# One table load, six pieces of gamma and a first store in two halves, in an RMSNorm that repeats its rows

## The chip, the cores and the metric

One core of one Trainium2 chip. The metric is the time of one execution on the device in microseconds (us), as the median of several; before the change it was 239.42 us (3 runs, 239.32 to 239.43). The span in a profile is about 1.8 us shorter than the time of the same run (237.9 and 239.72 us for the kernel before).

## The reference

(shortened)

```python
def reference(x, gamma):                       # x: 8 x 512 x 2048, gamma: 2048, both f32
    x_rep = np.repeat(x, 2, axis=1)            # every row twice
    rms = np.sqrt((x_rep ** 2).mean(axis=-1, keepdims=True) + 1e-6)
    return (x_rep / rms * gamma[None, None, :]).astype(np.float32)
```

33.6 MB are read and 67.1 MB written.

## The kernel before

Eight tiles of 128 partitions x 4 rows. A tile buffer has room for the eight output rows of a partition; the four input rows are loaded into its second half, normalised, and copied. SyncE issues every load of x and every store, ScalarE issues the loads of gamma and takes squares and roots, GpSimd copies gamma to all 128 partitions, VectorE scales, and each of the two copies half of the repeats. Three tile buffers are used in turn.

```python
    rows = ctx.enter_context(tc.tile_pool(name="rows", bufs=3))
    # ... cut
    def square(i, k):                            # ScalarE: sum of squares, then its root
        # ... cut
        nc.scalar.activation(out=sq[:], in_=ys[i][:, K * (R - 1) + k, :], func=Act.Square, accum_out=ss[:])
        nc.scalar.activation(out=rms[:], in_=ss[:], func=Act.Sqrt, scale=inv_d, bias=eps_t[:])
    # ... cut
    def compute(i):
        for k in range(K):
            scale(i, k, square(i, k))            # VectorE: reciprocal, then y * rstd * gamma_b
        repeat(i, 0, K // 2, nc.scalar.copy)
        repeat(i, K // 2, K, nc.vector.tensor_copy)

    load(0, nc.sync, parts=2)
    gamma_b = singles.tile([P, D], f32, name="gamma_b")
    cuts = [0, *range(D // 4, D + 1, D // 8)]    # seven pieces: 2 KB and six of 1 KB
    for c0, c1 in zip(cuts, cuts[1:]):
        nc.scalar.dma_start(out=gamma_b[0:1, c0:c1], in_=gamma[c0:c1].partition_broadcast(1))
    nc.gpsimd.partition_broadcast(out_ap=gamma_b[:], in_ap=gamma_b[0:1, :])
    # ... cut
    load(1, nc.sync)
    load(2, nc.sync)
    loads_after = {2: (3, 4, 5), 4: (6, 7)}
    for i in range(ntiles):
        compute(i)
        store(i, 0, K)
        for j in loads_after.get(i, ()):
            load(j, nc.sync)
```

Of the kernel before, what the change touches and what calls it, by code (L numbers as in the profile page):

```python
# [1 line left out]

# [4 lines left out]


@with_exitstack
def kernel(  # L10
    ctx: ExitStack,
    tc: tile.TileContext,
    x: bass.AP,
    gamma: bass.AP,
    out: bass.AP,
):
    nc = tc.nc
    P = nc.NUM_PARTITIONS
    f32 = mybir.dt.float32
    Act = mybir.ActivationFunctionType  # L20
    Alu = mybir.AluOpType

    B, S, D = x.shape
    Bo, So, Do = out.shape
    R = So // S
    assert R == 2 and D == Do and B == Bo and So == S * R
    eps = 1e-6
    inv_d = 1.0 / float(D)


    K = 4
    N = B * S
    assert N % (P * K) == 0
    ntiles = N // (P * K)
    x_t = x.rearrange("b s d -> (b s) d").rearrange("(n p k) d -> n p k d", p=P, k=K)
    out_t = out.rearrange("b s d -> (b s) d").rearrange("(n p j) d -> n p (j d)", p=P, j=K * R)

    singles = ctx.enter_context(tc.tile_pool(name="singles", bufs=1))
    rows = ctx.enter_context(tc.tile_pool(name="rows", bufs=3))
    junk = ctx.enter_context(tc.tile_pool(name="junk", bufs=1, space=bass.MemoryType.PSUM))  # L40
    small = ctx.enter_context(tc.tile_pool(name="small", bufs=8))

    ys = []

    def load(i, eng, parts=1):


        y = rows.tile([P, K * R, D], f32, name="y")
        step = K // parts
        for k in range(0, K, step):  # L50
            at = K * (R - 1) + k
            eng.dma_start(out=y[:, at : at + step, :], in_=x_t[i, :, k : k + step, :])
        ys.append(y)

    def store(i, k0, k1):
        nc.sync.dma_start(  # L56
            out=out_t[i, :, R * k0 * D : R * k1 * D],
            in_=ys[i][:, R * k0 : R * k1, :].rearrange("p j d -> p (j d)"),
        )

    def square(i, k):
        sq = junk.tile([P, D], f32, name="sq")
        ss = small.tile([P, 1], f32, name="ss")
        nc.scalar.activation(  # L64
            out=sq[:], in_=ys[i][:, K * (R - 1) + k, :], func=Act.Square, accum_out=ss[:]
        )
        rms = small.tile([P, 1], f32, name="rms")
        nc.scalar.activation(out=rms[:], in_=ss[:], func=Act.Sqrt, scale=inv_d, bias=eps_t[:])  # L68
        return rms

    def scale(i, k, rms):
        rstd = small.tile([P, 1], f32, name="rstd")
        nc.vector.reciprocal(out=rstd[:], in_=rms[:])  # L73
        nc.vector.scalar_tensor_tensor(  # L74
            out=ys[i][:, R * k, :], in0=ys[i][:, K * (R - 1) + k, :], scalar=rstd[:], in1=gamma_b[:],
            op0=Alu.mult, op1=Alu.mult,
        )

    def repeat(i, k0, k1, copy):
        y_r = ys[i].rearrange("p (k r) d -> p k r d", r=R)  # L80
        copy(out=y_r[:, k0:k1, 1, :], in_=y_r[:, k0:k1, 0, :])  # L81

    def compute(i):
        for k in range(K):
            scale(i, k, square(i, k))
        repeat(i, 0, K // 2, nc.scalar.copy)
        repeat(i, K // 2, K, nc.vector.tensor_copy)


    ctx.enter_context(tc.manual_schedule())  # L90
    load(0, nc.sync, parts=2)
    gamma_b = singles.tile([P, D], f32, name="gamma_b")
    cuts = [0, *range(D // 4, D + 1, D // 8)]
    for c0, c1 in zip(cuts, cuts[1:]):
        nc.scalar.dma_start(out=gamma_b[0:1, c0:c1], in_=gamma[c0:c1].partition_broadcast(1))  # L95
    nc.gpsimd.partition_broadcast(out_ap=gamma_b[:], in_ap=gamma_b[0:1, :])  # L96
    eps_t = singles.tile([P, 1], f32, name="eps_t")
    nc.vector.memset(eps_t, eps)  # L98
    load(1, nc.sync)
    load(2, nc.sync)  # L100



    assert ntiles == 8
    loads_after = {2: (3, 4, 5), 4: (6, 7)}
    for i in range(ntiles):
        compute(i)
        store(i, 0, K)
        for j in loads_after.get(i, ()):
            load(j, nc.sync)  # L110


# [1 line left out]
_INS = ['x', 'gamma']  # L114
_OUTS = [((8, 1024, 2048), 'float32')]


# [23 lines left out]
```

## Time and profile before

| | value |
|---|---|
| time | 239.42 us |
| profiled span | 237.9 us |
| VectorE, ScalarE busy | 96.5 us, 101.0 us |
| queue of x and of the stores, share of 16 DMA engines | 98.5% |
| first scaling starts, first store is issued | 14.92 us, 27.05 us |

The lines of the profile that carry the argument are in the prediction below. One view is not shown there: whom SyncE's DMA queue itself waited for (line that waited, what it waited for, us in total, times, longest).

```profile
SPq L52 <- DMA out_dram<-y: 69.6, 5, 19.1
SPq L52 <- DMA y<-in_x_dram: 5.7, 1, 5.7
SPq L52 <- DMA gamma_b<-in_gamma_dram: 0.9, 1, 0.9
```

L52 issues the loads of x. The first row is reuse of tile buffers. The other two cannot be: the first three tiles have fresh buffers, and a load of x needs no gamma. They are waits for a semaphore that a transfer shares with an earlier one. The list of instructions of the built kernel shows eight such semaphores, given to the DMAs in turn; a transfer that is given one again is issued only when the earlier transfer with it has landed.

### The profile page before, as it was taken

Reading aid. Unit: us, or ns where it says so; the run is one execution under the profiler, and the core shown is the slowest. Engines: PE = TensorE matmul, PEld = TensorE weight load, DVE = VectorE, ACT = ScalarE, POOL = GpSimd, SP = SyncE. Lnnn points to the kernel's source line nnn. Section 1 sums busy time; section 2 is a strip of 40 time slices with the busy share of each in tenths; the row PEclk is TensorE's granted clock in tenths of the full one; section 3 lists DMA queues with packets and bytes.
Section 4 is the critical chain, followed back from the end, with each engine's and each line's share of the span. In section 5 each row is a group of like instructions: output and inputs, shape, how many; then the busy total and the mean of one; then the engine's idle time right before and its main releaser. Section 6 shows DMA issues by size and latency. Waiting matters only on the chain.

```text
span 237.9 us, 287 instructions
## 1 busy us (share of the span) xinstructions
DVE 96.5 (41%) x73; ACT 101.0 (42%) x106; POOL 2.5 (1%) x5
## 2 busy tenths in 40 slices
DVE  0049999960000000059999960000199990000000
ACT  2697999900000000099999920000599960000000
POOL 0030000000000000000000000000000000000000
DMA  7999998989899998999998999989998989999994
GB/s 265 436 446 441 441 441 353 530 353 496 386 452 430 397 485 353 441 441 441 441 518 364 464 419 430 452 369 430 435 518 364 518 364 485 397 452 430 408 474 176
DMA packets 2464, 100.69 MB, mean 423 GB/s; under 512 B 279, under 2 KB 285, under 8 KB 286
## 3 DMA queue, kind: packets, MB, share of 16 engines
q1 hardware_dynamic: 2448, 100.66, 98.5%
q14 instruction: 2, 0.02, 0.0%
q10 hardware_dynamic: 14, 0.01, 0.0%
HBM read 33.56 MB, written 67.11 MB: 423 GB/s over the span
## 4 chain that ended last, share of the span: by engine, by line
DMA 58%; ACT 12%; DVE 9%; issue 1%; POOLq 1%; ACTq 1%; SPq 0%
DMA y<-in_x_dram 33%; DMA out_dram<-y 21%; ACT sq L64 8%; DVE y L74 7%; DMA gamma_b<-in_gamma_dram 4%; ACT y L81 3%; DVE y L81 2%; ACT rms L68 1%; POOLq L136 1%; ACTq L95 1%; DVE rstd L73 0%; POOLq L96 0%; SPq L56 0%
## 5 line engine op out<-in xcount | busy, mean ns | idle before, releaser
L64 ACT ACTIVATE sq<-y 128x2048 f32<-128x2048 f32 x32 | 59.7, 1865 | 87.8 <-DMA y<-in_x_dram 87.8
L74 DVE SCALAR_TENSOR_TENSOR y<-y,rstd,gamma_b 128x2048 f32<-128x2048 f32 x32 | 75.3, 2352 | 4.1 <-POOL gamma_b L96 3.0
L73 DVE RECIPROCAL rstd<-rms 128x1 f32<-128x1 f32 x32 | 5.0, 158 | 94.6 <-ACT rms L68 94.3
L81 ACT COPY y<-y 128x4096 f32<-128x4096 f32 x8 | 28.7, 3590 | 1.4 <-DVE y L74 1.4
L81 DVE COPY y<-y 128x4096 f32<-128x4096 f32 x8 | 18.3, 2294 | 0.3
L68 ACT ACTIVATE rms<-ss,eps_t 128x1 f32<-128x1 f32 x32 | 9.4, 295 | 1.0
L64 ACT ACTIVATION_READ_ACCUMULATOR sq<-y 128x1 f32 x32 | 6.0, 187 | 0.0
L64 ACT ACT_TABLE_LOAD x1 | 1.3, 1283 | 3.0 <-issue 3.0
L96 POOL PARTITION_BROADCAST gamma_b<-gamma_b x1 | 2.3, 2294 | 12.2 <-DMA y<-in_x_dram 12.2
L68 ACT ACT_TABLE_LOAD x1 | 1.3, 1283 | 0.0
L98 DVE MEMSET eps_t<- 128x1 f32 x1 | 0.1, 59 | 0.8 <-PEq L125 0.8
L125 POOL MEMSET const-uint8-127<- 128x1 uint8 x1 | 0.1, 102 | 0.0
L125 POOL MEMSET const-bfloat16-1.0<- 128x1 bf16 x1 | 0.1, 101 | 0.0
L125 POOL MEMSET const-float32-0.0<- 128x1 f32 x1 | 0.1, 98 | 0.2 <-issue 0.2
L125 POOL MEMSET const-float32-1.0<- 128x1 f32 x1 | 0.1, 98 | 0.0
## 6 DMA issues: line engine op xcount, KB each, us to landing
y<-in_x_dram SPq DMA_DIRECT2D x7, 4096.0 KB, 14.6
y<-in_x_dram SPq DMA_DIRECT2D x2, 2048.0 KB, 7.4
out_dram<-y SPq DMA_DIRECT2D x8, 24.4
gamma_b<-in_gamma_dram ACTq DMA_DIRECT2D x6, 1.0 KB
gamma_b<-in_gamma_dram ACTq DMA_DIRECT2D x1, 2.0 KB
```

Source lines behind the costliest of these rows:

```text
L64: nc.scalar.activation(out=sq[:], in_=ys[i][:, K * (R - 1) + k, :], func=Act.Square, accum_out=ss[:])
L68: nc.scalar.activation(out=rms[:], in_=ss[:], func=Act.Sqrt, scale=inv_d, bias=eps_t[:])
L73: nc.vector.reciprocal(out=rstd[:], in_=rms[:])
L74: nc.vector.scalar_tensor_tensor(out=ys[i][:, R * k, :], in0=ys[i][:, K * (R - 1) + k, :], scalar=rstd[:], in1=gamma_b[:], op0=Alu.mult, o ...
L81: copy(out=y_r[:, k0:k1, 1, :], in_=y_r[:, k0:k1, 0, :])
L95: nc.scalar.dma_start(out=gamma_b[0:1, c0:c1], in_=gamma[c0:c1].partition_broadcast(1))
L96: nc.gpsimd.partition_broadcast(out_ap=gamma_b[:], in_ap=gamma_b[0:1, :])
L98: nc.vector.memset(eps_t, eps)
L125: nc = _bacc.Bacc("TRN2", target_bir_lowering=False, num_devices=1)
L136: with _tile.TileContext(nc) as tc:
```

## The change

The intent: the square and the root use one function table, loaded at the start; gamma comes in one piece less; the first store need not wait until the whole tile is done.

```diff
     load(0, nc.sync, parts=2)
+
+    nc.scalar.preload_act_table(Act.Sqrt)
     gamma_b = singles.tile([P, D], f32, name="gamma_b")
-    cuts = [0, *range(D // 4, D + 1, D // 8)]
+    cuts = [0, D // 4, *range(D // 2, D + 1, D // 8)]
@@
         compute(i)
-        store(i, 0, K)
+
+        for k0, k1 in ((0, K // 2), (K // 2, K)) if i == 0 else ((0, K),):
+            store(i, k0, k1)
```

## The prediction

> **What bounds the kernel now.** I read the page first: engine shares, the slices, the DMA queues.
>
> ```profile
> DVE 96.5 (41%) x73; ACT 101.0 (42%) x106; POOL 2.5 (1%) x5
> ...
> DMA  7999998989899998999998999989998989999994
> ...
> q1 hardware_dynamic: 2448, 100.66, 98.5%
> q14 instruction: 2, 0.02, 0.0%
> q10 hardware_dynamic: 14, 0.01, 0.0%
> HBM read 33.56 MB, written 67.11 MB: 423 GB/s over the span
> ```
>
> The two compute engines are busy for about 41% of the span. The q1 row, the queue of SyncE with all loads of x and all stores, fills 98.5% of the time of the 16 DMA engines. So 0.985 x 237.9 = 234.4 us of the span is transfer, and only 3.5 us is anything else. Next I asked for busy time in stretches chosen to lie on the phases:
>
> ```profile
> 0.00:1.50 1.50, 0.06 (x1) 0.00 (x0) 0.19 (x4) 1.00 0.00 0
> 1.50:3.00 1.50, 0.00 (x0) 0.02 (x1) 0.00 (x0) 1.00 0.93 220
> 3.00:12.00 9.00, 0.17 (x1) 5.12 (x6) 0.00 (x0) 1.00 1.00 428
> ...
> 31.00:89.00 58.00, 20.04 (x15) 16.98 (x17) 0.00 (x0) 1.00 1.00 434
> 3.00:235.00 232.00, 96.48 (x72) 101.00 (x106) 2.29 (x1) 1.00 1.00 433
> ```
>
> The last two columns are the DMA share and GB/s. From 3 to 235 us the share is 1.00 at 433 GB/s: there is no hole in which a store or a load could have started earlier. In the packet records of the trace the first packet of x begins at 1.74 us and the last packet of a store ends at 236.77 us, 235.03 us apart, against 234.37 us of packet time per engine. All holes inside the stream together are 0.66 us per engine. The first instruction on the queue is issued at 0.72 us, so the rest is 1.0 us from issue to first packet and 1.2 us after the last packet.
>
> The chain of waits, read third, seems to say something else for the start:
>
> ```profile
> 2.69 9.71 DMA gamma_b<-in_gamma_dram
> ...
> 12.55 2.35 POOLq L136
> ...
> 14.92 2.35 DVE y L74
> ...
> 24.69 2.30 DVE y L81
> ...
> 27.05 25.77 DMA out_dram<-y
> 52.82 0.02 issue
> 52.84 48.32 DMA y<-in_x_dram
> ```
>
> It runs through gamma, its broadcast and VectorE to the first store. But the store's 25.77 us are not all transfer: it has 8.39 MB (67.11 MB over 8 stores), which at 434 GB/s is 19.3 us. The other 6.4 us it stands in the queue behind the loads of tiles 1 and 2, about 1 us of it being the issue. The last load of those lands at 33.3 us by its semaphore. So the first store has some 5 us of slack, and the piece of the chain ahead of it is not on the path that sets the end. The chain shows who released whom, not that the engines of the DMA were idle.
>
> **What the Trainium skill says.** "DMA: Bandwidth & Descriptors", Specifications, gives a fabric ceiling of 435 GB/s; the 434 GB/s of 31 to 89 us agrees. It also gives about 358 GB/s for the HBM share of a core; the page's 423 GB/s of reads and writes together is above that, and the measurement decides. The same page, "Issuing engines are not separate DMA queues", says that DMAs issued by ScalarE and SyncE run on the same 16 engines; and "Queues, rings and completion order" says that an engine takes turns between its queue rows packet by packet. The records of q10 agree: 14 packets for seven pieces of gamma, each a data packet and a semaphore packet, and from the second piece on (5.65 us) the two are 0.65 us apart, about one packet of x of 16 KB (0.61 us). "ScalarE: Activation LUTs", "What ACT_TABLE_LOAD costs", gives about 1.28 us for a load and 1.38 us for the drain[...]; the trace has the 1.28 us, but between the end of the first square's read-out (9.94 + 0.19) and the first square root (11.43) there is room for the load alone:
>
> ```profile
> 9.94 0.19 ACT L64 ACTIVATION_READ_ACCUMULATOR sq<-y 128x1 f32 x1
> 10.14 1.28 ACT L68 ACT_TABLE_LOAD   x1
> 11.43 0.29 ACT L68 ACTIVATE rms<-ss,eps_t 128x1 f32<-128x1 f32 x1
> 11.64 1.86 ACT L64 ACTIVATE sq<-y 128x2048 f32<-128x2048 f32 x1
> ```
>
> **The change part by part.** I compared the instruction order of the two built kernels.
>
> Table load. Two loads become one: the square and the square root now share the set loaded first. The load at 10.14 us goes, 1.28 us off ScalarE, so the first square root starts at about 10.15. On the path: nothing. VectorE's first scaling waits for gamma until 14.92, while its reciprocal was done at 11.93.
>
> Gamma. ScalarE loads its table at about 0.72 to 2.0 and issues six pieces after it: in the trace seven took 2.23 us including one of 0.51, so six take 1.7 to 2.0 us and end near 3.9. Before, the first piece (2 KB) got in ahead of x, at 1.62 us, and the other six ran from 5.65 to 12.01, that is 6.36 us. Now all six stand behind x. If their turns start at 5.65 as before, they end at 12.0; if the 1.3 us of later issue carries over in full, at 13.3, and somewhat later when packets of 32 KB (1.21 us) follow those of 16 KB. I take 12 to 14. The broadcast (2.3 us) then ends at 14.9 to 16.5, and tile 0 is done on VectorE 0 to 1.6 us later than before: its last store issue moves from 27.05 to 27.0 to 28.7. All inside the 5 us of slack.
>
> Semaphores. The order list shows eight semaphores given to DMAs in turn. Before, the second half of the first load had to wait for the first piece of gamma (the trace: 0.9 us, issue at 2.03); now gamma comes later in the turn, so both halves go out one after the other near 0.72 and 1.1. The first half has 2.1 MB, 4.8 us of work, so its engines weren't waiting for the second half. Load of tile 1 still waits for the first half to land (8.11). Seven pieces and one store became six and two, so from the second store on every transfer has the same semaphore as before. The sixth piece costs nothing elsewhere.
>
> First store. It goes in two: the first as soon as ScalarE has copied rows 0 and 1 of each partition (19.77 + 3.60 = 23.37, up to 1.6 later), the second when VectorE is done. Both still queue behind load 2. Bytes are the same; 128 packets of 64 KB become 256 of 32 KB. From the packet records: 2.418 us for 64 KB and 1.213 for 32 KB, so two halves cost 8 ns more than one whole. Eight such per engine are 0.06 us, with one more semaphore packet of 9 ns: 0.07 us. The load into that buffer needs the second half to have landed, whose last byte comes in the same place in the stream (52.82 us).
>
> Sum on the end: 0.0 from the table, 0.0 from gamma, +0.07 from packets, and 0 to -0.3 if the start becomes cleaner with ScalarE issuing nothing in the first microsecond. That is 239.42 + 0.07 - 0.1 = about 239.4 us.
>
> **Rivals.**
> 1. The chain is right and the start is on the path: the table load, 1.28 us, and the first half store 3.6 us earlier come off the end. That makes 235.8 to 238.1. For it: the chain of waits. Against it: the DMA share of 1.00 from 3 us on, and the 6.4 us that the first store already stands in the queue. Even if all holes went, only 0.66 us could come.
> 2. Gamma's later issue delays tile 0 beyond the slack. It would have to come more than 5 us later, after 17 us, since everything behind it follows rigidly. For it: gamma takes turns with x on one engine, and turns get twice as long (1.21 us) with tile 1's packets. Six pieces of two turns at 1.21 us would be 14.5 us and end at about 20, 8 us late: an undivided first store would go out at 35, and the stream, whose loads run out near 32.5, would stand still for some 3.5 us. Divided, its first half goes out at 31.4 and its first packet at 32.4, just in time, with 9.7 us of work in it, and the hole is 0 to 1 us: 239.4 to 240.4. Against so late a gamma: 16 packets of 16 KB are in the ring of that engine for the first load, and they last till about 12 us, so few turns are the long ones.
> 3. Shorter store packets cost more than I count: if 32 KB writes behaved as the 16 KB reads (0.611 us each, 1% worse), 0.2 us on 19.3. That would be 239.6.
> 4. The start is cleaner: 0.3 to 0.6 us of the 0.66 us of holes go, 238.9 to 239.1.
>
> **Range and chances.** The runs of before lie within 0.11 us of each other. Rivals 3 and 4 span 238.9 to 239.6; with some difference between chips I take 238.8 to 240.0 for 8 in 10, at 239.4. A change of 2% is 4.8 us: faster by it would need more than all holes of the stream together (chance 0.01), slower by it needs a dry queue of 5 us, far beyond rival 2 (0.02). Within 2%: 0.97.
>
> **What would show it.** In the profile after: one table load of 1.28 us, at the start; the first square root at 10.1 to 10.2; the broadcast starting between 12.3 and 14; the first store's first half issued at 23.4 to 25, the second at 27 to 28.7; the load of tile 3 still issued at about 52.8; q1 at 2,592 packets (2448 + 128 + 16) and again about 98.5%; the share 1.00 in the stretch from 3 to 235. I am wrong if the stretch from 28 to 40 us shows less than full share (rival 2), if the load of tile 3 goes out more than 1 us earlier or later, or if 434 GB/s of the steady stretch changes.

## The result, and the profile after

The changed kernel takes 239.57 us (median of 6 runs, 239.42 to 239.79), the kernel before 239.43 (6 runs, 239.32 to 239.63). The ratio is 1.0006, with a 95% interval of 0.9993 to 1.0019: the same. A ratio, here and below, is the mean time of one kernel's fast runs over that of the other's of the same rounds, so it is not quite the ratio of the medians.

First the page of the kernel after, shares and DMA queues:

```profile
DVE 96.5 (41%) x73; ACT 99.9 (42%) x105; POOL 2.5 (1%) x5
...
q1 hardware_dynamic: 2592, 100.66, 98.6%
q14 instruction: 2, 0.02, 0.0%
q10 hardware_dynamic: 12, 0.01, 0.0%
```

ScalarE lost the 1.1 us of the table load net, the main queue has 144 packets more, gamma's queue two fewer, and the main queue is as full as it was. The stretches (length, busy time of VectorE, ScalarE, GpSimd, TensorE clock, DMA share, GB/s) answer to those of before:

```profile
3.00:12.00 9.00, 0.16 (x1) 3.98 (x4) 0.87 (x1) 1.00 1.00 428
31.00:89.00 58.00, 18.61 (x13) 16.28 (x17) 0.00 (x0) 1.00 1.00 434
3.00:235.00 232.00, 96.46 (x72) 98.66 (x104) 2.29 (x1) 1.00 1.01 432
```

Same share, same rate. What did change is the first tile, in the timeline after (start, duration, engine, line, operation):

```profile
0.72 1.28 ACT L93 ACT_TABLE_LOAD   x1 [0.72 <-PEq L129]
...
0.75 1.93 ACTq L97 DMA_DIRECT2D gamma_b<-in_gamma_dram  x6
...
11.13 2.29 POOL L98 PARTITION_BROADCAST gamma_b<-gamma_b  x1 [10.71 <-DMA gamma_b<-in_gamma_dram]
...
13.46 2.35 DVE L74 SCALAR_TENSOR_TENSOR y<-y,rstd,gamma_b 128x2048 f32<-128x2048 f32 x1 [2.95 <-POOL gamma_b L98]
...
21.93 3.95 SPq L56 DMA_DIRECT2D out_dram<-y  x2
```

The broadcast starts at 11.13 instead of 12.60, the first scaling at 13.46 instead of 14.92, and the store goes out at 21.93 and 25.54 instead of 27.05. So the first tile is 1.5 us ahead, and its first half store 5.1 us. In the chain of waits after, the first store's piece has grown by what the pieces ahead of it lost, and the load of tile 3 follows at 52.96 (before: 52.84):

```profile
25.54 27.36 DMA out_dram<-y
52.96 48.24 DMA y<-in_x_dram
```

The second half holds 4.19 MB, 9.7 us at 434 GB/s, and takes 27.36 us to land. The 1.5 us are given back in the queue, one for one. In the packet records the first packet of x starts at 1.74 us and the last one of a store ends at 236.68 us; before, 1.74 and 236.77. None of the three signs of being wrong that the prediction names came: from 28 to 40 us the share is 0.99, tile 3 goes out 0.12 us later, and the steady rate is 434 GB/s.

### The profile page after: what moved, and what is told of

Its sections match the earlier page's. It is cut to its first block, busy times and chain, and to the rows that moved or that the text cites. A ratio compares the mean times of both kernels' runs of the same rounds, so it can differ in the third digit from the quotient of the medians.

```text
span 237.8 us, 285 instructions
## 1 busy us (share of the span) xinstructions
DVE 96.5 (41%) x73; ACT 99.9 (42%) x105; POOL 2.5 (1%) x5
## 4 chain that ended last, share of the span: by engine, by line
DMA 58%; ACT 12%; DVE 9%; issue 2%; POOLq 1%; ACTq 0%; SPq 0%
DMA y<-in_x_dram 32%; DMA out_dram<-y 22%; ACT sq L64 8%; DVE y L74 7%; DMA gamma_b<-in_gamma_dram 4%; ACT y L81 3%; DVE y L81 2%; ACT rms L68 1%; POOLq L140 1%; ACTq L97 0%; DVE rstd L73 0%; ACT L93 0%; POOLq L98 0%; SPq L52 0%
## 5 line engine op out<-in xcount | busy, mean ns | idle before, releaser
L81 ACT COPY y<-y 128x4096 f32<-128x4096 f32 x8 | 28.7, 3591 | 0.9 <-DVE y L74 0.9
```

The costliest lines, as they stand in the source:

```text
L81: copy(out=y_r[:, k0:k1, 1, :], in_=y_r[:, k0:k1, 0, :])
```

## The experiments

All were run beside the kernel before on the same chip, twelve in four groups. Times are medians; the interval is that of the ratio to the kernel before. Theory A ("stream"): the DMA engines are never empty, so nothing in the first tile counts until it makes them empty. Rival B ("start on the path"): what the chain of waits shows ahead of the first store is paid in full.

**The early table load undone.**

```diff
-    nc.scalar.preload_act_table(Act.Sqrt)
```

> The changed kernel without the early table load, so ScalarE loads two tables again (2 x 1.28 us). Stream theory (the DMA engines are never empty, so work of the first tile costs nothing): first square root back at about 11.3 us instead of 10.02, first scaling still at about 13.5 because gamma gates it, time 239.5 within 0.2 of the changed kernel. Rival, start on the path: 1.3 us more than the changed kernel, 240.8. If gamma's landing was helped by the issue order and not by the number of pieces, the broadcast would move from 11.13 towards 12.6; by the number of pieces it stays at about 11.1.

239.38 us against 239.33, ratio 0.9998 (0.9985 to 1.001). The broadcast and the first root:

```profile
11.27 2.29 POOL L97 PARTITION_BROADCAST gamma_b<-gamma_b  x1 [10.84 <-DMA gamma_b<-in_gamma_dram]
11.38 0.29 ACT L68 ACTIVATE rms<-ss,eps_t 128x1 f32<-128x1 f32 x1
```

The root is late again, and gamma is not; the first scaling starts at 13.59. So the table load is worth nothing to the end, and it is not what brought gamma forward; that leaves the number of pieces. (The build gave out the semaphores differently here too: the load of tile 1 is issued at 2.01 us and not at 7.98. The end did not follow that either.)

**Gamma in seven pieces again.**

```diff
-    cuts = [0, D // 4, *range(D // 2, D + 1, D // 8)]
+    cuts = [0, *range(D // 4, D + 1, D // 8)]
```

> The changed kernel with the seven pieces of gamma of before. If each piece costs two turns of 0.61 to 0.65 us on one DMA engine, the last packet of gamma ends at about 11.8 to 12.0 instead of 10.57, the broadcast starts at about 12.4 and the whole of the first tile moves 1.3 us later: store halves at about 23.2 and 26.9. If instead the early table load brought gamma forward, the broadcast stays at about 11.1. Time by the stream theory 239.5 as before; by the rival (start on the path) 1.3 us more, 240.8.

242.10 us against 239.33, ratio 1.0113 (1.0099 to 1.0127). Neither theory expected this size, and gamma moved the other way: its broadcast started at 8.97 us. Something else had happened. SyncE's waits in this run (same columns as above), and its issues in the timeline near 8 us:

```profile
SPq L52 <- DMA y<-in_x_dram: 6.9, 1, 6.9
```

```profile
0.73 0.38 SPq L52 DMA_DIRECT2D y<-in_x_dram  x1
```

```profile
8.08 0.33 SPq L52 DMA_DIRECT2D y<-in_x_dram  x1
```

Between the first half of the first load, at 0.73, and the second half, at 8.08, SyncE issues nothing. In the built kernel the two halves have the same one of the eight semaphores: the first half takes one, gamma's seven pieces take the other seven, and the second half is given the first again, so it must wait until the first half has landed. By then the stream is empty. Stretches of this run, then of the changed kernel:

```profile
7.75:9.15 1.40, 0.00 (x0) 1.07 (x1) 0.17 (x1) 1.00 0.38 82
```

```profile
7.75:9.15 1.40, 0.00 (x0) 1.16 (x1) 0.00 (x0) 1.00 1.07 457
```

(A packet is counted where it starts, so the share of a short stretch is coarse and can pass 1.) In the packet records no packet of x is in flight from 7.72 to 9.05 us; idle time per engine between 7 and 12 us is about 1.8 us, against none in the changed kernel. The first packets after the pause take 0.7 to 1.4 us instead of 0.61; packet time per engine is 0.6 us more in all. Together 2.4 us, and the span is 2.4 us longer (240.2 against 237.8). This also explains gamma: while x had nothing in the ring (the queue of packets that stand ready for a DMA engine), four pieces went through from 7.54 to 7.74 us, 0.05 us each, where one beside x takes 1.26.

**Seven pieces, but the table load after them.** If the explanation is right, moving one instruction must mend it. Against the previous run:

```diff
-    nc.scalar.preload_act_table(Act.Sqrt)
     # ... cut
     for c0, c1 in zip(cuts, cuts[1:]):
         nc.scalar.dma_start(...)
+    nc.scalar.preload_act_table(Act.Sqrt)
```

> Seven pieces and two half stores as in the run with seven pieces that took 242.1, but the early table load stands after the issues of gamma instead of ahead of them. In the build the second half of the first load then waits for the semaphore of the first piece of gamma (landed at about 2 us), as in the kernel before, and no longer for that of the first half of the same load (landed at 8.1). Shared semaphore theory: no hole near 8 us, the second half issued at about 2.0, gamma's last packet at about 12.0, first scaling near 14.8, time 239.5 (239.2 to 239.9). If seven pieces with two half stores were themselves the cost: 242.1 again.

239.75 us against 239.57, ratio 1.0013 (0.9997 to 1.0029). With the table load behind them, the build gives gamma's first piece its semaphore ahead of the first half, and the second half shares with that piece, which lands early. SyncE's waits and the stretch of before:

```profile
SPq L52 <- DMA gamma_b<-in_gamma_dram: 0.9, 1, 0.9
```

```profile
7.75:9.15 1.40, 0.00 (x0) 1.08 (x1) 0.00 (x0) 1.00 0.93 399
```

Same pieces, same half stores, no hole. It also gives the measure of a piece: from the start of its second piece to the end of its last packet gamma takes 6.37 us with seven pieces (5.54 to 11.91; the same in the kernel before) and 5.14 with six (5.42 to 10.57 in the changed kernel). One piece less is 1.2 us.

**Gamma in one piece.**

```diff
-    cuts = [0, D // 4, *range(D // 2, D + 1, D // 8)]
+    cuts = [0, D]
```

> The changed kernel with gamma in one piece of 8 KB. The first piece has always gone ahead of the first packet of x (1.66 against 1.74 us), so all of gamma should land by about 2.5 to 3 us, the broadcast runs at about 3, the first scaling is gated by the first square root only and starts at about 10.5, the store halves are issued at about 19 and 22.6. Time by the stream theory still 239.4 within 0.2. By the rival (start on the path) 3 us less, 236.5. If one packet of 8 KB cannot go ahead of x, gamma lands at about 6 to 7 us.

239.75 us against 239.33, ratio 1.0016 (1.0003 to 1.0028). Broadcast and first scaling:

```profile
2.86 2.29 POOL L98 PARTITION_BROADCAST gamma_b<-gamma_b  x1 [2.43 <-DMA gamma_b<-in_gamma_dram]
10.76 2.35 DVE L74 SCALAR_TENSOR_TENSOR y<-y,rstd,gamma_b 128x2048 f32<-128x2048 f32 x1
```

The single packet of 8 KB went ahead of x at 1.66 us, as expected, and the first scaling came 4.2 us earlier than in the kernel before. The halves were issued at 21.09 and 22.84; I had expected 19 for the first, and overlooked that ScalarE copies only after its four squares, the third of which waits for the second half load (13.0 us). The end did not gain, and rival B is out.

**No gamma at all** (wrong result: ones in place of gamma).

```diff
-    cuts = [0, D // 4, *range(D // 2, D + 1, D // 8)]
-    for c0, c1 in zip(cuts, cuts[1:]):
-        nc.scalar.dma_start(...)
-    nc.gpsimd.partition_broadcast(...)
+    nc.vector.memset(gamma_b, 1.0)
```

> Wrong result on purpose: gamma is set to ones on VectorE, no transfer and no broadcast. First scaling at about 10.5. Stream theory: 239.4 within 0.3 (8 KB of bytes less count nothing). Rival, start on the path: at least 3 us less, 236.5.

239.77 us against 239.33, ratio 1.0016 (1.0002 to 1.0029), with the first scaling at 10.50. The same verdict. That these two runs lie 0.4 us above the kernel before is more than I expected, and both intervals lie just above 1. The kept traces do not show why: their last store packets end at 236.79 and 236.60 us, against 236.77 in the kernel before. The cause stays open.

**Only the split undone.**

```diff
-        for k0, k1 in ((0, K // 2), (K // 2, K)) if i == 0 else ((0, K),):
-            store(i, k0, k1)
+        store(i, 0, K)
```

> The changed kernel with only the split of the first store undone. The store is issued at about 25.5, and the loads run dry at 31.5 to 32 when no store stands behind them (as the run with the delay of 9.4 us and a whole store showed), so its first packet at 26.5 to 27 is in time by 5 us. Expected 239.4 (239.1 to 239.8), the same as with halves, with 128 x-ring packets fewer. If the halves were worth anything without a delay: above 240.

239.89 us against 239.57, ratio 1.0008 (0.9996 to 1.002); the median is 0.1 us above the range expected. The halves are worth nothing measurable when the first tile is in time.

**How much slack the first store has.** Four runs delay the first tile with idle scalings on VectorE, with the store whole or in halves:

```diff
+            if i == 0 and k == 0:
+                for _ in range(4):               # or 7
+                    nc.vector.scalar_tensor_tensor(out=pad[:], in0=gamma_b[:], scalar=rms[:], in1=gamma_b[:], ...)
```

(The runs with a whole store have the split undone as well, as in the run above.)

Four scalings, store whole:

> The changed kernel with the first store whole, and four idle scalings (about 2.35 us each, 9.4 in all) on VectorE ahead of the first tile's. The store would be issued at about 34.9 instead of 25.5; its first packet starts about 1.0 us later, at 35.9, while load 2 lands at 33.3. Slack theory: the stream has a hole of about 2.6 us, time 242.1 (241.3 to 242.7). If the start is on the path in full: 9.4 more, 248.9. If the slack is larger than I read: 239.5.

Four scalings, store in halves:

> The same delay of 9.4 us with the first store in halves. First half issued at about 31.3, its first packet at 32.3, before load 2 has landed (33.3), and it holds 9.7 us of work, until the second half is issued at 34.9. Slack theory: no hole, 239.5 (up to 239.9): the halves are worth about 2.6 us here. If halves are worth nothing: the same as the whole store with this delay.

Seven scalings, store whole:

> First store whole, delay of seven idle scalings, 16.5 us. Issued at about 42, first packet 43, load 2 landed at 33.3: a hole of 9.7 us, time 249.2 (248 to 250), that is 7.1 more than with the delay of 9.4: past the slack each us of delay costs one us.

Seven scalings, store in halves:

> First store in halves, delay of 16.5 us. First half issued at about 38.4, first packet 39.4, hole of 6.1 us, the second half comes in time behind it: 245.6 (244.6 to 246.5). So the halves are worth 3.6 us once the delay is past both slacks, which is the time between ScalarE's copy and VectorE's last work on the tile.

| delay | store | issued at | stream empty | time, us | ratio to before (95%) |
|---|---|---|---|---|---|
| 9.6 us | whole | 35.21 | 31.87 to 36.06 | 245.05 | 1.0229 (1.0214 to 1.0245) |
| 9.6 us | halves | 31.68, 35.29 | 31.85 to 32.53 | 241.37 | 1.007 (1.0054 to 1.0087) |
| 16.7 us | whole | 42.68 | 32.02 to 43.54 | 252.24 | 1.0531 (1.0515 to 1.0546) |
| 16.7 us | halves | 39.12, 42.73 | 32.10 to 39.97 | 248.62 | 1.038 (1.0365 to 1.0396) |

"Stream empty" is the time in which the packet records show no packet of x or of a store. The stretches of the two runs with the shorter delay, the whole store first:

```profile
32.00:36.00 4.00, 3.93 (x4) 3.94 (x7) 0.00 (x0) 1.00 0.00 0
```

```profile
32.00:36.00 4.00, 3.93 (x4) 3.94 (x6) 0.00 (x0) 1.00 0.92 393
```

The shape came out as expected: past the slack each us of delay costs one us (7.2 us for 7.2), and the halves are worth 3.7 and 3.6 us, the time between the two issues. The sizes were off by 3.0 us and 1.9 us at the shorter delay and by 3.0 us in both runs at the longer one; all four times lie above the ranges expected. Two things were missing. The loads run dry at 31.9 us, not at 33.3: in the kernel before, the last packets of the load (to 33.01 us) share the engines with packets of a store already in the ring (from 32.41 us). Its records have 0.87 us of stretched packets in the ten us from 30 on, against 0.05 in the run with the empty ring. And both delayed runs have about 0.9 us of packet time more than the kernel before, in packets that took up to 3.5 us for 64 KB. They lie near 92 and 122 us with the whole store, near 88 and 119 with the halves, each time at the end of a row of stores or loads, where the other kind follows; the records of before show almost none at these turns. For the whole store: 4.4 us of idle per engine between 25 and 50 us and 0.9 us of longer packets are 5.3 us, and the span is 5.3 us longer. Why those later packets stretch stays open.

**Store packets of 16 KB everywhere.**

```diff
-        for k0, k1 in ((0, K // 2), (K // 2, K)) if i == 0 else ((0, K),):
-            store(i, k0, k1)
+        for h in range(R):                       # R is 2; each transfer: runs of 16 KB, every second one
+            nc.sync.dma_start(
+                out=out_t[i].rearrange("p (a h c d) -> h p a (c d)", a=2, h=2, c=2)[h],
+                in_=ys[i].rearrange("p (a h c) d -> h p a (c d)", a=2, h=2, c=2)[h])
```

> The changed kernel with every store in two transfers, each with runs of 16 KB (four packets where there was one of 64 KB). From the reads' packet times (0.611 us for 16 KB, 2.418 for 64 KB) one run of 64 KB costs 0.026 us more in four pieces; 64 such per engine (56 for the whole stores, and 8 less the 0.008 each for the first) make 1.6 us, with semaphore packets 1.7: 241.2 (240.8 to 241.6). If smaller store packets cost nothing: 239.5. If writes pay more per packet than reads: above 241.6.

240.91 us against 239.47, ratio 1.0056 (1.0042 to 1.007). Of the 4,096 store packets of 16 KB, 4,090 took 0.611 us, as the reads do, so four cost 2.444 against 2.418 us for one of 64 KB: the 0.026 us that I had worked with. The 1.4 us at the end are a little less than the 1.6 to 1.7 worked out from it, near the lower end of the range. The queue of x and of the stores in this run, as its page has it:

```profile
q1 hardware_dynamic: 5648, 100.66, 98.8%
```

With over twice the packets of the kernel before, the cost is 1.4 us. So the 144 packets that the change adds can't be seen.

**Half of the first store left out** (wrong result).

```diff
-        for k0, k1 in ((0, K // 2), (K // 2, K)) if i == 0 else ((0, K),):
+        for k0, k1 in ((K // 2, K),) if i == 0 else ((0, K),):
```

> Wrong result on purpose: the first half of the first store is left out, 4.19 MB of 100.66. If the end is set by the bytes through the 16 engines at 434 GB/s, 9.66 us less than the changed kernel: 229.9 (229.6 to 230.3), if the stream stays without holes: the second half is issued at 25.5, before load 2 has landed. If the end were set by compute or by the chain from the first tile: 239.5.

230.14 us against 239.47, ratio 0.961 (0.959 to 0.963).

```profile
q1 hardware_dynamic: 2448, 96.47, 98.5%
...
HBM read 33.56 MB, written 62.91 MB: 423 GB/s over the span
```

4.19 MB less is 9.3 us less than the kernel before on the same chip (9.4 against the changed kernel), where 9.7 were worked out from 434 GB/s; the four runs spread over 1.1 us, and the profiled span is 9.8 us shorter than that of the changed kernel. The end follows the bytes. No version here beats the kernel before: all those with full bytes and no hole, the one with packets of 16 KB apart, lie between 239.4 and 239.9 us.

## Why the prediction was right or wrong

**The bound: right.** Dropping bytes moves the end, dropping the whole path of gamma doesn't. 3 to 235 us are at full share after, too. Rival 1 is refuted by the runs with one piece and without gamma. (Two sums in the text are slips that change nothing: 0.985 x 237.9 is 234.3, not 234.4, and with both of its gains off the end rival 1 would come to 234.5, not 235.8.) What holds the stream at 434 GB/s, the engines or the memory behind them, no run here separates.

**The table load: right.** First root at 10.02 us; nothing at the end, as the run without it showed.

**Gamma: wrong in direction, harmless.** The step that failed is "ScalarE loads its table at about 0.72 to 2.0 and issues six pieces after it". The issues run from 0.75 us on, beside the table load; the first piece still goes ahead of x at 1.66. So "Now all six stand behind x" was wrong too: five do, where six did before. The broadcast came 1.5 us earlier (11.13), where 12.3 to 14 was expected, and the two half stores went out at 21.93 and 25.54, ahead of the expected 23.4 to 25 and 27 to 28.7. Of the 1.5 us the missing piece is 1.2; the rest is an earlier second piece (5.42 instead of 5.65 us), whose start lies anywhere from 5.39 to 5.77 in the runs with six pieces. The time at the end came out right in spite of this step, because gamma does not reach the end either way. Two turns of 0.61 to 0.65 us for a piece, as expected for the run with seven, was right: 1.2 between seven and six, 1.26 from one piece to the next.

**Semaphores: right for what was built, but read too narrowly.** "The sixth piece costs nothing elsewhere" holds. What I missed is that a seventh would: with the table load ahead of the issues and seven pieces, the two halves of the first load share a semaphore, and that costs 2.8 us by the medians of the same chip (242.10 against 239.33), 2.4 by the profiled spans. The parts of this change aren't independent. The list of semaphores that I had read for the changed kernel would have shown it for that variant.

**The first store: right at the end, the slack mis-sized.** "Some 5 us of slack" came from the landing of load 2 at 33.3 us. With an empty ring behind it the load's data ends at 31.9, and a store's first packet follows its issue by 0.84 us in all four delayed runs (about 1 was taken), so the issue may come by about 31.0: 4 us after 27.05. The halves guard against delays, as rival 2 said, and past the slack they are worth 3.6 us. Without a delay they are worth nothing.

**Packets: right.** 0.07 us was expected, and is too small to see (the packet time per engine of the two profiled runs differs by 0.18 us, 0.11 of it in stretched packets); the run with 16 KB everywhere gives it a scale. **A cleaner start (rival 4): not seen at the end**; the first packet of x starts at 1.74 us in both. The holes inside the stream went from 0.66 to 0.40 us per engine in the profiled runs, but they lie between 0.25 and 0.68 in the other runs without an empty stream and packets of 16 KB, and do not follow any part of the change.

## What to carry to other kernels

When one transfer queue is at full share from start to end, work that is taken off ahead of it is only turned into queueing: look at the share in stretches before the chain of waits, and test it by leaving out bytes. What can still cost time is anything that empties the queue, and a change that only shifts the count or the order of small transfers can do that, if transfers share semaphores in turn: after such a change read, for every early issue, which earlier transfer it waits for. Splitting a store buys slack, not time; measure the slack with a deliberate delay before paying for it.

## What the Trainium skill lacked or had wrong

- "DMA: Bandwidth & Descriptors", Specifications: about 358 GB/s stands in the table as the HBM limit of a core, half of a stack's 716. For this program on one core that row is no limit: it held 434 GB/s of reads or writes from 31 to 89 us, and the fabric ceiling of 435 GB/s in the same table fits. The page is not wrong in this, as it says further down that 358 is what each gets when both cores of a pair stream; the row alone does not say it.
- "DMA: Bandwidth & Descriptors", Queues, rings and completion order: a turn is said to be 9 to 17 descriptors typically. Here a transfer of gamma and its semaphore each waited 0.6 us, one record of 16 KB of x per turn, which makes a piece cost 1.26 us beside x and 0.05 us beside an empty ring. Whether such a record is a descriptor or a packet of the page, the trace does not say.
- "ScalarE: Activation LUTs", What ACT_TABLE_LOAD costs: the drain of 1.38 us that the page adds to every switch wasn't seen; from the end of the read-out (10.13) to the first root (11.43) lie 1.3 us, the load alone. The page doesn't say that DMA issues of the same engine go on during a load, which they do here (load 0.72 to 2.00, issues from 0.75 on).
- None of the pages that I read says what it costs when two transfers are given the same semaphore in a build: here a wait of 6.9 us, an empty stream of 1.3 us and 2.4 to 2.8 us at the end.
- None of them says that the last packets of a load can stretch where a store follows: 0.87 us per engine in the ten us from 30 on, with a store already in the ring, 0.05 without. In the delayed runs it comes at later turns instead, where the kernel before has almost none, so what decides it stays open.
